# Queries and keys of an attention kernel: transposed in fp32 and split into parts from PSUM

## The chip, the core and the metric

The kernel runs on one core of a Trainium2 chip. A core has a matrix engine, TensorE (PE in the profile; its weight loads are listed apart as PEld), three engines for elementwise work, VectorE (DVE), ScalarE (ACT) and GpSimd (POOL), and a queue, SyncE (SP), that issues the DMAs here. PE writes only to PSUM, from which DVE and ACT read. The metric is the device time of one execution in microseconds (us), lower is better.

## The reference

One inference step of a four-layer backbone with 640 tokens (128 context tokens and 512 latent ones) of width 1024, 16 query heads and 4 key heads of 64. What matters of a layer:

```python
u = rms_norm(h, norm_pre[l]) * (1 + scl) + shift
p = u @ w_in_l
q, k, v, z = split(p)                       # 16 heads of q, 4 of k and v, gate z
q = rms_norm(q, q_g); k = rms_norm(k, k_g)  # per head
q, k = apply_rope(q), apply_rope(k)         # layers 0, 1 and 3, latent tokens
s = einsum('bqhgd,bkhd->bhgqk', q * scale, k)
o = softmax(s) @ v                          # over latent keys and cached context keys
h = h + gate * rms_norm((o * silu(z)) @ w_out_l, norm_post[l])
```

Layers 0 and 3 attend to all keys, layer 1 to a band, layer 2 to a neighbourhood on a grid. The 128 context tokens attend only to themselves; their keys and values are outputs too. The keys of an earlier context come from the input `cache_k`.

## The kernel before

Everything is fp32. A matrix product is made of products in the matrix engine's type F32R: a value is split into a high part, rounded to F32R, and a low part, the rest. For the scores the parts lie on the 128 rows that PE sums over: a query head of 64 is stacked as 64 rows of high parts and 64 rows of low parts, and a key head lies twice on the 128 rows, once in high parts (`kst[:, g, 0]`) and once in low parts (`kst[:, g, 1]`). So two matmuls per block of scores sum all four products.

A layer runs in stages: keys and values of five token tiles of 128 (`kv_chunk`); then two chunks of 8 query heads. A chunk makes its queries tile by tile (`q_chunk`: projection L497, headnorm, rotation, and then the parts), the gate `z` (L634), the attention of four pairs of heads (scores L698 or L724, transposed probabilities L773, product with values L780) and the heads of the context tokens (L800, L826, L834). The second chunk has two other key heads: their six tiles are stacked into `kst` anew (L1000), from `kn2`, where `kv_chunk` kept them. There is one buffer `kst` at a time; the output phase (L901 and what follows) borrows it for its gate rows. Last comes the output projection.

How parts are made before: for a query tile (L610 to L623), twice four heads, ACT rounds them into the first half of `hl` (L613), DVE or POOL subtracts to get the low parts into the other half (L615), PE transposes the four heads of 128 columns in F32R (L620), and ACT or DVE copies 512 elements per row from PSUM to the query tile `q` (`evac`, L256). For a key tile (`k_stack`, L538) ACT rounds two heads, doubled by a broadcast (L544), DVE or POOL subtracts (L545), PE transposes four pieces of 128 columns in F32R (L553), and ACT or DVE copies 512 elements to `kst`.

The order of the work is not written by hand. `Sched.emit` (L126) is a planner that runs when the program is built: each operation has a list of engines it may run on with an assumed duration, the operations it depends on, the buffers it needs, and a priority; the planner takes the one that can start first and emits a fixed order for each engine. PSUM is given out as two double tiles `S` and four tiles `B` (L227); tiles `cap_...` limit how much is in flight. Durations `P(336, tr, "R")`, `As(256, ...)` and the like are the planner's, in ns and elements. Each engine then executes its list in order and waits on semaphores.

## Time and profile before

| | |
|---|---|
| median of 3 runs | 1398.39 us (1394.93 to 1403.29) |
| the profiled execution | 1400.58 us, its span 1398.5 us |
| PE busy | 1357.7 us, 97% |
| DVE busy | 954.7 us, 68% |
| ACT busy | 758.6 us, 54% |
| POOL busy | 266.8 us, 19% |
| mean share of the DMA engines busy | 32% |
| mean granted clock of PE | 0.998 |

The profile is of one execution. The busy time of an engine is the union of its instructions; PE's matmuls overlap, so a listed duration of one of them is longer than what it adds, which is seen from the starts of the runs that follow each other in the timeline. A line of the page's part 5 or of the groups says how long an engine was idle just before those instructions and which instruction ended that wait.

### The profile page before, as it was taken

How to read it: one execution, taken by the hardware profiler on the slowest of the kernel's cores; microseconds unless marked ns; L12 is line 12 of the kernel's file. 1: busy time of each engine (PE TensorE's matmuls, PEld its weight loads, DVE VectorE, ACT ScalarE, POOL GpSimd, SP SyncE). 2: the span in 40 equal slices, each digit the busy share in tenths (PEclk: the TensorE clock that was granted, in tenths of full speed). 3: DMA queues.
4: the chain of work that ended last, by engine and by line, in shares of the span. 5: the costliest groups of instructions: out<-in, count | busy, mean ns of one | idle time of the engine just before them, and what ended most of it. 6: DMA issues, size and time to landing. Idle time of an engine off the chain costs nothing.

```text
span 1398.5 us, 25496 instructions
## 1 busy us (share of the span) xinstructions
PE 1357.7 (97%) x9464; PEld 1122.3 (80%) x9464; DVE 954.7 (68%) x2300; ACT 758.6 (54%) x1854; POOL 266.8 (19%) x306
## 2 busy tenths in 40 slices
PE   6999999999999999999999999999999999999998
PEld 3788887888778887887878888888778888778876
DVE  4777667765587786777486676578488876577653
ACT  4556565554355565666354567468345555465641
POOL 1122012010032102201033541441033210021100
PEclk9999999999999999999999999999999999999999
DMA  8522222224532402324542522342633210111032
GB/s 305 175 69 84 61 91 84 69 87 140 181 115 67 147 30 91 125 92 161 161 125 73 157 57 91 98 141 85 196 126 101 91 53 10 61 52 41 31 123 103
DMA packets 73323, 145.11 MB, mean 104 GB/s; under 512 B 8752, under 2 KB 13936, under 8 KB 73200
## 3 DMA queue, kind: packets, MB, share of 16 engines
q1 hardware_dynamic: 73200, 143.50, 31.6%
q8 instruction: 74, 1.21, 0.4%
...
## 4 chain that ended last, share of the span: by engine, by line
PE 83%; DVE 6%; ACT 4%; DMA 3%; issue 3%; POOL 0%; SPq 0%; DVEq 0%; POOLq 0%; ACTq 0%
PE B L497 21%; PE B L634 14%; PE B L780 8%; PE B L773 8%; PE S L901 8%; PE B L901 6%; PE S L698 5%; PE S L724 4%; PE B L383 3%; PE B L620 2%; PE S L497 1%; DVE w L262 1%; DMA raw<-in_w_mod 1%; DMA raw<-in_w_in 1%; PE B L451 1%
## 5 line engine op out<-in xcount | busy, mean ns | idle before, releaser
L307 POOL TENSOR_TENSOR sm<-sm,mhalf 128x1 f32<-128x1 f32 (+2 forms) x100 | 122.1, 1223 | 573.2 <-DVE sm L302 291.5
L497 PE MATMUL B<-w,uB 128*128 128x512 f32 x816 | 207.4, 401 | 0.0
L256 ACT ACTIVATE pt<-B 128x512 f32<-128x512 f32 (+1 forms) x228 | 126.9, 570 | 121.0 <-PE B L773 110.8
L497 PEld LDWEIGHTS B<-w,uB 128*128 128x128 f32 x816 | 149.2, 188 | 31.8 <-DVE uB L262 0.4
L634 PE MATMUL B<-uB,w 128*128 128x384 f32 x768 | 166.0, 348 | 0.6 <-DVE gate L642 0.3
L773 PE MATMUL B<-ident,p 128*128 128x128 f32 x1088 | 159.4, 276 | 3.1 <-ACT pt L256 2.3
L261 ACT ACTIVATE w<-raw 128x512 fp32r<-128x512 f32 x224 | 135.0, 627 | 30.2 <-PE B L901 8.0
L773 PEld LDWEIGHTS B<-ident,p 128*128 128x128 f32 x1088 | 125.1, 141 | 23.7 <-issue 13.6
L262 DVE TENSOR_TENSOR w<-raw,w 128x512 fp32r<-128x512 f32 x193 | 130.5, 700 | 13.0 <-ACT w L261 12.4
L497 PE MATMUL B<-w,uA 128*128 128x512 f32 x528 | 135.1, 403 | 1.1 <-DVE pt L256 0.8
L703 ACT ACTIVATE p<-S,sm 128x640 f32<-128x640 f32 x128 | 101.3, 794 | 59.6 <-DVE sm L701 54.6
L780 PE MATMUL B<-pt,vt 128*64 128x256 f32 (+1 forms) x1152 | 133.0, 376 | 0.0
L634 PEld LDWEIGHTS B<-uB,w 128*128 128x128 f32 x768 | 129.6, 188 | 3.7 <-issue 1.5
L701 DVE TENSOR_REDUCE sm<-S 128x1 f32<-128x640 f32 x128 | 102.7, 819 | 37.7 <-PE S L698 36.8
L634 PE MATMUL B<-uA,w 128*128 128x256 f32 x768 | 117.6, 290 | 0.3 <-DVE modc L394 0.3
L497 PEld LDWEIGHTS B<-w,uA 128*128 128x128 f32 x528 | 96.4, 188 | 24.7 <-DVE w L262 2.1
L780 PEld LDWEIGHTS B<-pt,vt 128*64 128x64 f32 x1152 | 77.5, 137 | 46.0 <-issue 11.4
L634 PEld LDWEIGHTS B<-uA,w 128*128 128x128 f32 x768 | 102.5, 189 | 3.4 <-issue 1.8
L658 DVE TENSOR_SCALAR p<-p,sm 128x640 f32<-128x640 f32 (+2 forms) x197 | 96.9, 506 | 6.6 <-DVE sm L657 0.5
L698 PE MATMUL S<-kst,q 128*128 128x320 f32 x512 | 96.8, 320 | 2.9 <-ACT p L703 2.8
L658 POOL TENSOR_SCALAR p<-p,sm 128x640 f32<-128x640 f32 (+2 forms) x59 | 44.0, 751 | 284.3 <-DVE sm L657 236.4
L737 ACT ACTIVATE p<-p,sm 128x512 f32<-128x512 f32 (+1 forms) x128 | 83.9, 657 | 6.4 <-DVE sm L735 6.3
...
## 6 DMA issues: line engine op xcount, KB each, us to landing
...
```

The costliest lines, as they stand in the source:

```text
L256: alts = {"A": Ap(n, lambda e: e.activation(out(), in_(), AF.Copy)), "V": V(n, lambda e: e.tensor_copy(out(), in_()))}
L261: S.op([As(n, lambda e: e.activation(h(), src(), AF.Copy))], r, w)
L262: f = lambda e: e.tensor_sub(l(), src(), h().bitcast(F32))
L307: S.op([("G", 395 + 157 * n, lambda e: e.tensor_tensor(r.ap, v.ap, mhalf.ap.to_broadcast([128, n]), op=OP.pow), "pow")], r=[v, mhalf], w=[r])
L497: e.matmul(ps(), t.ap[:, s, k, off:off + 128], W[k].ap[:, w], start=k == 0 and i == 0, stop=k == 7 and i == 2)
L634: e.matmul(ps.ap[:, 0:w], W[k].ap[:, wi, 128 * f:128 * f + 128], t.ap[:, s, k, :], start=k == 0 and i == 0, stop=k == 7 and i == 2)
L658: f = lambda e, i=i, p=p, w=w: e.tensor_scalar(p.ap[:, 0:w], p.ap[:, 0:w], rs.ap[:, i:i + 1], 1.0, op0=OP.mult, op1=OP.mult)
L698: e.matmul(ps.ap[:, b, 0:320], Q[t + 1].ap[:, hh], kst.ap[:, g, s, 320 * b:320 * b + 320], start=s == 0, stop=s == 1)
L701: S.op([V(640, lambda e, ps=ps, i=i: e.tensor_reduce(negm.ap[:, i:i + 1], ps.ap[:, :, 0:320], axis=AX.XY, op=OP.max, negate=True))], r=[ps ...
L773: e.transpose(pt.ap[:, c:c + 128], p.ap[:, b:b + 128], ident.ap)
L780: e.matmul(po.ap[64 * x:64 * x + 64, 256 * half + q0:256 * half + q0 + w], vt.ap[:, kt, 64 * g:64 * g + 64], sbt.ap[:, c0:c0 + w], start=f ...
L901: e.matmul(ps(), t.ap[:, s, k, off:off + 128], W[k].ap[:, w], start=k == 0 and i == 0, stop=k == 7 and i == 2)
```

## The change

For queries: the tile is transposed first, in fp32, four transposes of two heads each (128 columns) into one PSUM tile. After that head `2r` lies on partitions 0 to 63 and head `2r+1` on 64 to 127. For the even heads (x = 0), ACT rounds the 64 partitions out of PSUM into the upper 64 partitions of `q`, and DVE subtracts that from PSUM and writes the low part to the other 64 partitions. For the odd heads high and low part change places; both halves of a key are the same, so scores are computed as before. A score instruction now waits for the even or odd heads of its tile, instead of the first or second four.

For keys: the source is now the two heads doubled side by side, so that one transpose of 128 columns gives a head on both halves. The cached keys are loaded twice by DMA for that, `kn2` holds doubled heads, and a new copy `kd` (ACT or DVE) doubles the others. PE transposes two pieces of 128 columns in fp32 instead of four in F32R; ACT rounds 256 elements per row from PSUM into `kst`, and DVE subtracts into the low part.

```diff
--- before.py
+++ after.py
@@ -538,32 +538,28 @@
     @S.named("ks")
     def k_stack(src, srckey, kst, ct, cap=None):
 
-        hl = tmp([128, 2, 2, 2, 64], F32R)
         tc_ = [cap, kst] if cap else [kst]
-        s = lambda: src()[:, :, None, :].to_broadcast([128, 2, 2, 64])
-        S.op([As(256, lambda e: e.activation(hl.ap[:, 0], s(), AF.Copy))], r=[srckey], w=[(hl, 0)], touch=tc_)
-        f = lambda e: e.tensor_sub(hl.ap[:, 1], s(), hl.ap[:, 0].bitcast(F32))
-        S.op([G(256, f), VL(256, f)], r=[srckey, (hl, 0)], w=[(hl, 1)], touch=tc_)
-        ps = S.buf("B", [128, 512], F32R)
+        ps = S.buf("B", [128, 512])
 
         def tr(e):
-            for i in range(2):
-                for g in range(2):
-                    c = 128 * (2 * i + g)
-                    e.transpose(ps.ap[:, c:c + 128], hl.ap[:, i, g].rearrange("p a d -> p (a d)"), identr.ap)
-        S.op([P(336, tr, "R")], r=[hl, identr], w=[ps], touch=tc_)
-        evac(512, lambda: kst.ap[:, :, :, 128 * COL[ct]:128 * COL[ct] + 128],
-             lambda: ps.ap.bitcast(F32).rearrange("p (i g c) -> p g i c", i=2, g=2), [ps], [(kst, ct)])
+            for g in range(2):
+                e.transpose(ps.ap[:, 128 * g:128 * g + 128], src()[:, g].rearrange("p a d -> p (a d)"), ident.ap)
+        S.op([P(218, tr, "T")], r=[srckey, ident], w=[ps], touch=tc_)
+        v = lambda: ps.ap[:, 0:256].rearrange("p (g c) -> p g c", g=2)
+        d = lambda i: kst.ap[:, :, i, 128 * COL[ct]:128 * COL[ct] + 128]
+        S.op([As(256, lambda e: e.activation(d(0), v(), AF.Copy))], r=[ps], w=[(kst, ct)])
+        S.op([V(256, lambda e: e.tensor_sub(d(1), v(), d(0).bitcast(F32)))], r=[ps, (kst, ct)], w=[(kst, ct)])
 
     def new_kst():
         return S.buf("kst", [128, 2, 2, 768], F32R)
 
     @S.named("kv")
     def kv_chunk(l, tabs, W):
-        kst, vt, kn2 = new_kst(), S.buf("vt", [128, 6, 256]), S.buf("kn2", [128, 6, 2, 64])
-        ck = tmp([128, 2, 64])
-        S.op([D(64, lambda e: e.dma_start(ck.ap, a["cache_k"][0, l, :, 0:2]))], w=[ck], touch=[kst])
-        S.op([D(64, lambda e: e.dma_start(kn2.ap[:, 4], a["cache_k"][0, l, :, 2:4]))], w=[(kn2, 4)])
+        kst, vt, kn2 = new_kst(), S.buf("vt", [128, 6, 256]), S.buf("kn2", [128, 6, 2, 2, 64])
+        ck = tmp([128, 2, 2, 64])
+        for x in range(2):
+            S.op([D(64, lambda e, x=x: e.dma_start(ck.ap[:, :, x], a["cache_k"][0, l, :, 0:2]))], w=[(ck, x)], touch=[kst])
+            S.op([D(64, lambda e, x=x: e.dma_start(kn2.ap[:, 4, :, x], a["cache_k"][0, l, :, 2:4]))], w=[(kn2, 4)])
         S.op([D(128, lambda e: e.dma_start(vt.ap[:, KC, :], a["cache_v"][0, l].rearrange("t h d -> t (h d)")))], w=[(vt, KC)])
         k_stack(lambda: ck.ap, ck, kst, 4)
         for tau in range(5):
@@ -588,9 +584,13 @@
             if tau == 0:
                 S.op([D(128, lambda e, kn=kn: e.dma_start(o["nk"][0, l], kn.ap))], r=[kn])
                 S.op([D(128, lambda e: e.dma_start(o["nv"][0, l].rearrange("t h d -> t (h d)"), vt.ap[:, VC, :]))], r=[(vt, VC)])
-            S.op([As(128, lambda e, kn=kn, ct=ct: e.activation(kn2.ap[:, ct], kn.ap[:, 2:4], AF.Copy))], r=[kn], w=[(kn2, ct)],
+            two = lambda k0, kn=kn: kn.ap[:, k0:k0 + 2, None, :].to_broadcast([128, 2, 2, 64])
+            S.op([As(256, lambda e, two=two, ct=ct: e.activation(kn2.ap[:, ct], two(2), AF.Copy))], r=[kn], w=[(kn2, ct)],
                  touch=[cap])
-            k_stack(lambda kn=kn: kn.ap[:, 0:2], kn, kst, ct, cap)
+            kd = tmp([128, 2, 2, 64])
+            S.op([As(256, lambda e, two=two, kd=kd: e.activation(kd.ap, two(0), AF.Copy)),
+                  V2(256, lambda e, two=two, kd=kd: e.tensor_copy(kd.ap, two(0)))], r=[kn], w=[kd], touch=[cap, kst])
+            k_stack(lambda kd=kd: kd.ap, kd, kst, ct, cap)
         return kst, vt, kn2
 
     @S.named("qt")
@@ -607,20 +607,20 @@
                 qn = rope(xr, 8, tabs, "q", tau - 1, cap)
             else:
                 qn = gscale(xr, 8, tabs, 0, cap)
-            for i in range(2):
-                hl, pt = tmp([128, 4, 128], F32R), S.buf("B", [128, 512], F32R)
-                s = lambda i=i, qn=qn: qn.ap[:, 4 * i:4 * i + 4]
-                S.op([As(256, lambda e, s=s, hl=hl: e.activation(hl.ap[:, :, 0:64], s(), AF.Copy))], r=[qn], w=[(hl, 0)],
-                     touch=[cap])
-                f = lambda e, s=s, hl=hl: e.tensor_sub(hl.ap[:, :, 64:128], s(), hl.ap[:, :, 0:64].bitcast(F32))
-                S.op([G(256, f), VL(256, f)], r=[qn, (hl, 0)], w=[(hl, 1)], touch=[cap])
-
-                def tr(e, hl=hl, pt=pt):
-                    for h in range(4):
-                        e.transpose(pt.ap[:, 128 * h:128 * h + 128], hl.ap[:, h], identr.ap)
-                S.op([P(336, tr, "R")], r=[hl, identr], w=[pt], touch=[cap])
-                evac(512, lambda i=i, q=q: q.ap[:, 4 * i:4 * i + 4].rearrange("p h t -> p (h t)"),
-                     lambda pt=pt: pt.ap.bitcast(F32), [pt], [(q, i)])
+            pt = S.buf("B", [128, 512])
+
+            def tr(e, pt=pt, qn=qn):
+                for pr in range(4):
+                    e.transpose(pt.ap[:, 128 * pr:128 * pr + 128], qn.ap[:, 2 * pr:2 * pr + 2].rearrange("p h d -> p (h d)"),
+                                ident.ap)
+            S.op([P(436, tr, "T")], r=[qn, ident], w=[pt], touch=[cap])
+            for x in range(2):
+                hi, lo = (slice(0, 64), slice(64, 128))[::1 - 2 * x]
+                d = lambda rows, x=x, q=q: q.ap.rearrange("p (r x) t -> p x r t", x=2)[rows, x]
+                v = lambda hi=hi, pt=pt: pt.ap[hi].rearrange("p (r t) -> p r t", r=4)
+                S.op([As(512, lambda e, d=d, v=v, hi=hi: e.activation(d(hi), v(), AF.Copy))], r=[pt], w=[(q, x)], touch=[cap])
+                S.op([V(512, lambda e, d=d, v=v, hi=hi, lo=lo: e.tensor_sub(d(lo), v(), d(hi).bitcast(F32)))], r=[pt, (q, x)],
+                     w=[(q, x)], touch=[cap])
             Q.append(q)
         return Q
 
@@ -697,7 +697,7 @@
...
-                S.op([P(588, mm)], r=[(Q[t + 1], hh // 4)] + [(kst, x) for x in range(5)], w=[ps], seq="s")
+                S.op([P(588, mm)], r=[(Q[t + 1], hh % 2)] + [(kst, x) for x in range(5)], w=[ps], seq="s")
...
@@ -798,7 +798,7 @@
...
-            S.op([P(880, mm)], r=[(Q[0], gg), (kst, 5)], w=[ps], seq="s")
+            S.op([P(880, mm)], r=[Q[0], (kst, 5)], w=[ps], seq="s")
...
```

The planner then gives another order. On PE, in the stage of layer 0 that makes the first chunk's queries, before (`tmp` is `hl`, `q` and `kst` are the scores' inputs):

```order
L497 MATMUL B<-w,uB 128x512 x21
L620 MATMUL B<-identr,tmp 128x128 x4
L497 MATMUL B<-w,uB 128x512 x3
L620 MATMUL B<-identr,tmp 128x128 x4
L497 MATMUL B<-w,uB 128x512 x18
L620 MATMUL B<-identr,tmp 128x128 x4
L497 MATMUL B<-w,uB 128x512 x3
L620 MATMUL B<-identr,tmp 128x128 x4
L497 MATMUL B<-w,uB 128x512 x3
L698 MATMUL S<-kst,q 128x320 x4
L497 MATMUL B<-w,uB 128x512 x9
```

and now (`tmp` is the rotated query tile):

```order
L497 MATMUL B<-w,uB 128x512 x15
L614 MATMUL B<-ident,tmp 128x128 x4
L497 MATMUL B<-w,uB 128x512 x21
L614 MATMUL B<-ident,tmp 128x128 x4
L497 MATMUL B<-w,uB 128x512 x9
L698 MATMUL S<-kst,q 128x320 x4
L497 MATMUL B<-w,uB 128x512 x12
L614 MATMUL B<-ident,tmp 128x128 x4
L497 MATMUL B<-w,uB 128x512 x9
L698 MATMUL S<-kst,q 128x320 x4
L497 MATMUL B<-w,uB 128x512 x6
```

Two groups of four transposes per token tile, with projection or other matmuls between them, became one group of four.

On PE at the start of layer 1, where the cached keys are stacked, before (`tmp` are the parts of key tiles):

```order
L497 MATMUL B<-w,uA 128x512 x12
L497 MATMUL B<-w,uB 128x512 x18
L553 MATMUL B<-identr,tmp 128x128 x4
L497 MATMUL B<-w,uB 128x512 x3
L553 MATMUL B<-identr,tmp 128x128 x4
L497 MATMUL B<-w,uB 128x512 x15
L451 MATMUL B<-ident,p 128x128 x8
```

and now (the first `tmp` is the DMA's tile of cached keys):

```order
L497 MATMUL B<-w,uA 128x512 x12
L546 MATMUL B<-ident,tmp 128x128 x2
L497 MATMUL B<-w,uB 128x512 x18
L546 MATMUL B<-ident,tmp 128x128 x2
L497 MATMUL B<-w,uB 128x512 x18
L451 MATMUL B<-ident,p 128x128 x8
L497 MATMUL B<-w,uB 128x512 x6
```

The first transposes of a key tile moved from behind the first 18 projection matmuls of `uB` to a place ahead of them. On SP the load of the cached keys stands in the same place, before:

```order
L959 DMA xs_4274<-q 128x1024
L322 DMA raw<-in_w_in 128x512 x2
L565 DMA tmp<-in_cache_k 128x128
L322 DMA raw<-in_w_in 128x512
L590 DMA out_nv<-vt 128x256
L589 DMA out_nk<-tmp 128x256
```

and now:

```order
L959 DMA xs_4149<-q 128x1024
L322 DMA raw<-in_w_in 128x512 x2
L561 DMA tmp<-in_cache_k 128x2x64 x2
L322 DMA raw<-in_w_in 128x512
L586 DMA out_nv<-vt 128x256
L585 DMA out_nk<-tmp 128x256
```

It became two DMAs, one after the other, between the same weight loads.

On PE at the second chunk's keys of layer 0, before:

```order
L800 MATMUL S<-kst,q 128x128 x8
L780 MATMUL B<-pt,vt 64x256 x10
L553 MATMUL B<-identr,tmp 128x128 x24
L834 MATMUL B<-pt,vt 64x128 x4
L383 MATMUL B<-raw,cpad 32x128 x16
```

and now (`kn_441` is the buffer `kn2`):

```order
L800 MATMUL S<-kst,q 128x128 x8
L780 MATMUL B<-pt,vt 64x256 x10
L546 MATMUL B<-ident,kn_441 128x128 x12
L834 MATMUL B<-pt,vt 64x128 x4
L383 MATMUL B<-raw,cpad 32x128 x16
```

24 F32R transposes in a row became 12 in fp32, in the same place, and they read `kn2` itself.

## Rows read from the trace of the kernel before

**Rows 1.** The page: part 1, the busy time of each engine with its share of the span and its instructions; and the first line of part 4, the chain of work that ended last by engine, in shares of the span.

```profile
PE 1357.7 (97%) x9464; PEld 1122.3 (80%) x9464; DVE 954.7 (68%) x2300; ACT 758.6 (54%) x1854; POOL 266.8 (19%) x306
...
PE 83%; DVE 6%; ACT 4%; DMA 3%; issue 3%; POOL 0%; SPq 0%; DVEq 0%; POOLq 0%; ACTq 0%
```

**Rows 2.** Windows by stage: the stretch in us from the span's start, its length, then for each engine the busy time and (x) its instructions, the granted clock of PE, the share of the DMA engines and GB/s. The first chunk of queries of layer 0, the attention that follows, and the stage of layer 0's second chunk of keys and queries.

```profile
84.00:116.00 32.00, 31.84 (x238) 28.11 (x241) 26.68 (x54) 19.67 (x42) 8.95 (x7) 1.00 0.31 100
116.00:193.00 77.00, 77.00 (x661) 66.37 (x651) 54.65 (x113) 48.51 (x113) 8.91 (x10) 1.00 0.20 63
193.00:246.00 53.00, 49.86 (x346) 40.91 (x342) 34.05 (x71) 26.71 (x61) 11.70 (x8) 1.00 0.27 89
```

**Rows 3.** Timeline of PE in the first query stage of layer 0: start in us, length of the merged run, engine, line, operation, output and inputs, shape, count. L497 are projection matmuls, L620 the F32R transposes of query parts, four to a group.

```profile
86.83 4.43 PE L497 MATMUL B<-w,uB 128*128 128x512 f32 x18
91.10 0.46 PE L620 MATMUL B<-identr,tmp 128*128 128x128 f32 x4
91.39 0.93 PE L497 MATMUL B<-w,uB 128*128 128x512 f32 x3
92.16 0.47 PE L620 MATMUL B<-identr,tmp 128*128 128x128 f32 x4
92.46 0.93 PE L497 MATMUL B<-w,uB 128*128 128x512 f32 x3
```

**Rows 4.** Timeline of PE at the start of layer 1, same columns; the last one of a line is the idle time before it and what ended that. L451 are fp32 transposes of normalized rows, four to a group; L497 with uA and uB are the projection of keys and values of the first two and the last three token tiles.

```profile
393.41 0.60 PE L451 MATMUL B<-ident,p 128*128 128x128 f32 x4
393.77 3.05 PE L497 MATMUL B<-w,uA 128*128 128x512 f32 x12
396.66 0.60 PE L451 MATMUL B<-ident,p 128*128 128x128 f32 x4
...
402.40 3.05 PE L497 MATMUL B<-w,uA 128*128 128x512 f32 x12
405.29 4.39 PE L497 MATMUL B<-w,uB 128*128 128x512 f32 x18
```

**Rows 5.** Groups of instructions by line and shape over the whole span: line, engine, operation, names, shapes, count | busy us, mean ns of one | idle before and what ended it. Splitting of queries (L613, L615) and keys (L545), their transposes (L620, L553) and copies out of PSUM (L256), and two DVE operations of 512 elements with (L510) and without (L528) an operand in PSUM.

```profile
L256 ACT ACTIVATE q<-B 128x512 fp32r<-128x512 f32 x78 | 45.0, 595 | 31.9 <-PE B L620 31.6
...
L620 PE MATMUL B<-identr,tmp 128*128 128x128 f32 x320 | 36.1, 243 | 3.0 <-ACT pt L256 1.4 <-DVE tmp L615 1.3 <-DVE gate L642 0.4
...
L615 DVE TENSOR_TENSOR tmp<-tmp 128x256 fp32r<-128x256 f32 x78 | 32.2, 435 | 12.9 <-ACT tmp L613 12.7
...
L613 ACT ACTIVATE tmp<-tmp 128x256 fp32r<-128x256 f32 x80 | 29.5, 410 | 68.1 <-DVE tmp L534 41.9 <-DVE tmp L528 26.0
...
L510 DVE TENSOR_TENSOR tmp<-B,sm 128x512 f32<-128x512 f32 x40 | 27.5, 688 | 41.0 <-POOL sm L307 40.9
...
L256 ACT ACTIVATE kst<-B 128x512 fp32r<-128x512 f32 x44 | 25.4, 597 | 14.1 <-PE B L553 13.4
...
L553 PE MATMUL B<-identr,tmp 128*128 128x128 f32 x192 | 21.9, 246 | 3.8 <-ACT pt L256 1.9 <-DVE gate L642 0.7 <-DVE sm L806 0.4
...
L528 DVE TENSOR_TENSOR tmp<-tmp 128x512 f32<-128x512 f32 x24 | 16.8, 699 | 0.3
...
L545 DVE TENSOR_TENSOR tmp<-kn,tmp 128x256 fp32r<-128x256 f32 x22 | 9.7, 504 | 0.0
...
L545 DVE TENSOR_TENSOR tmp<-tmp 128x256 fp32r<-128x256 f32 x23 | 9.6, 420 | 4.2 <-ACT tmp L544 4.0
```

**Rows 6.** Timeline around the cached key tile in layers 0 to 3, all engines, same columns: the DMA's issue on SP's queue (L565), ACT's rounding of that tile (L544), and in layers 2 and 3 the projection matmuls that PE was in.

```profile
37.47 0.33 SPq L565 DMA_DIRECT2D tmp<-in_cache_k  x1
...
43.09 0.42 ACT L544 ACTIVATE tmp<-tmp 128x256 fp32r<-128x256 f32 x1 [2.59 <-DMA tmp<-in_cache_k]
...
402.67 0.42 SPq L565 DMA_DIRECT2D tmp<-in_cache_k  x1
...
407.23 0.42 ACT L544 ACTIVATE tmp<-tmp 128x256 fp32r<-128x256 f32 x1 [1.28 <-DMA tmp<-in_cache_k]
...
725.43 0.43 SPq L565 DMA_DIRECT2D tmp<-in_cache_k  x1
...
727.01 2.98 PE L497 MATMUL B<-w,uB 128*128 128x512 f32 x12
...
728.77 0.42 ACT L544 ACTIVATE tmp<-tmp 128x256 fp32r<-128x256 f32 x1 [0.36 <-DMA tmp<-in_cache_k]
...
1049.60 0.42 SPq L565 DMA_DIRECT2D tmp<-in_cache_k  x1
...
1051.18 2.97 PE L497 MATMUL B<-w,uB 128*128 128x512 f32 x12
...
1052.62 0.42 ACT L544 ACTIVATE tmp<-tmp 128x256 fp32r<-128x256 f32 x1
```

**Rows 7.** Timeline of PE at the second chunk of keys in layer 3: L553 are the F32R transposes of keys, L780 the product of probabilities and values.

```profile
1191.76 0.53 PE L553 MATMUL B<-identr,tmp 128*128 128x128 f32 x4 [1.56 <-ACT pt L256]
1192.60 0.53 PE L553 MATMUL B<-identr,tmp 128*128 128x128 f32 x4 [0.30 <-ACT pt L256]
1193.05 3.76 PE L780 MATMUL B<-pt,vt 128*64 128x256 f32 x20
```

**Rows 8.** Two windows of 1 us there, with the columns of rows 2.

```profile
1191.00:1192.00 1.00, 0.24 (x3) 0.24 (x3) 1.00 (x4) 1.00 (x5) 0.00 (x0) 1.00 0.00 0
...
1194.00:1195.00 1.00, 1.00 (x8) 0.59 (x6) 0.05 (x1) 0.92 (x6) 0.00 (x0) 0.50 0.00 0
```

More of the change, by code (lines that the diff above doesn't have):

```diff
@@ L724, in mm @@
                             e.matmul(ps.ap[:, i, o:o + n], Q[t + 1].ap[:, hh], v(s), start=s == 0, stop=s == 1)
-                S.op([P(w * 0.88 + 14, mm)], r=[(Q[t + 1], hh // 4)] + [(kst, x) for x in BAND[t]], w=[(ps, i)], seq="s")
+                S.op([P(w * 0.88 + 14, mm)], r=[(Q[t + 1], hh % 2)] + [(kst, x) for x in BAND[t]], w=[(ps, i)], seq="s")
                 bb, bap = bias[t]
```

## The prediction

> **What bounds the kernel now.** I read the page's busy shares and chain of waits first, then the windows by stage, then TensorE's timeline inside three stages. The reader should see in [rows 1] that TensorE (PE) is busy for 97% of the span and holds 83% of the chain that ended last, while DVE (68%) and ACT (54%) have room. [rows 2] show the same in a stage: while the queries of layer 0 are made (84 to 116 us) PE is busy 31.84 of 32 us and DVE 26.68. So a us taken from PE counts nearly in full as long as PE isn't made to wait, and work that moves between DVE and ACT counts only where it makes PE wait. DVE at 83% in that stage is the engine to watch.
>
> **The change part by part.**
>
> PE, removed. A query tile needs two groups of four F32R transposes, a key tile one: 320 and 192 instructions [rows 5], so 80 and 48 groups. One group costs less than its listed 243 ns each suggests, because they overlap. In [rows 3] the matmuls behind a group begin 0.29 and 0.30 us after it began. The matmuls ahead of it tell whether it starts late: 18 take 4.27 us, 0.237 each, so three need 0.71, and three took 0.77. A group is 0.30 to 0.36 us; I take 0.31, since other stretches of this kind read as the lower end.
>
> PE, added. A query tile gets one group of four fp32 transposes, a key tile one of two: 40 groups and 48. The kernel before has fp32 transposes of the same size. In [rows 4] a group of four lets the next matmuls begin 0.36 us later (393.41 to 393.77); the 12 matmuls up to the next group took 2.89 us where 12 at 0.237 need 2.84, so the front costs 0.05, and up to 0.08 if the rate of other stretches is taken. That is 0.41 to 0.44, I take 0.435. A group of two is taken as half of that, 0.20 to 0.22; I take 0.22.
>
> The sum on PE: queries 40 x (2 x 0.31 - 0.435) = 7.4 us, keys 48 x (0.31 - 0.22) = 4.3 us, together **-12 us**. By the ends: 40 x (0.60 - 0.44) + 48 x (0.30 - 0.22) = 10 us, and 40 x (0.72 - 0.41) + 48 x (0.36 - 0.20) = 20 us.
>
> DVE and ACT. From [rows 5]: DVE loses 78 subtractions of a query's low part (32.2 us), 45 of a key's (19.3) and the six copies from PSUM that fell to it (6 x 0.69), 55.6 us in all. It gains 80 subtractions of 512 at 0.69 and 48 of 256 at 0.42, 75.4 us. The new order also puts some 20 pieces of optional work on it that POOL or ACT did, about 10 us at 0.5 to 0.7 each. So DVE rises by about 30 us, to some 984, 70% of the span. ACT loses 80 roundings of queries (29.5), 122 copies out of PSUM (45.0 + 25.4), 48 roundings of keys like the first (48 x 0.41) and 20 copies half as wide (an estimate of 0.3 each from the 410 ns of the full width), 126 us; it gains 80 x 0.595 for queries and 88 x 0.41 for keys, 84. It falls by about 40. I price both at nothing: in the attention stages (116 to 193 us) PE is busy all 77 us and DVE 54.65 [rows 2], and there is room. In a query stage five tiles add 5 x (2 x 0.69 - 2 x 0.435) = 2.6 us to DVE's 26.68 of 32, which makes 91%. What it costs if that cover is gone is the third rival. Operations on 64 partitions are not in this trace; what is bounded is the number of elements in a row, 512, and I take them as long as those of 128 partitions. Half the time would take 28 us from DVE and change PE by nothing.
>
> On that subtraction the trace shows 688 ns for 512 elements with an operand in PSUM and 699 ns for both in SBUF [rows 5], so I charge nothing for moving it to PSUM. The Trainium skill (Perfetto Trace Analysis, section Optimizing Scalar/DVE Operations) speaks against the change here: about 60 ns of access overhead for DVE on SBUF and 125 on PSUM. By it the 128 subtractions would cost 8 us more DVE time, an estimate from that page, and the third rival would have 38 us to draw on instead of 30; the rows don't agree.
>
> The wait that is added. Before, the cached key tile went from its DMA to ACT, then DVE, then PE. ACT could stand still for it without PE noticing. Now PE transposes the DMA's tile itself, so PE waits for the DMA, and all its queued matmuls wait behind that. The DMA can start only when the tile of keys is free, at the end of a layer, and there are now two in a row on SP, 0.42 us apart [rows 6]. From SP's issue to ACT's use it took 5.62 us in layer 0, 4.56 in layer 1, 3.34 in layer 2 and at most 3.02 in layer 3 [rows 6]. In layer 1 the order puts the transposes right behind the 12 matmuls of [rows 4], at 405.29 us; the first half lands near 407.2, the second 0.42 later: PE stands 2.3 us. In layers 2 and 3 they come behind six of the 12 matmuls that began at 727.01 and 1051.18 [rows 6], so at 728.4 and 1052.6; with 3.34 + 0.42 us the data is there at 729.2 and 1053.4: 0.8 us each. In layer 0 the second half is issued behind a 512 KB weight piece, about 41.4 us, and lands between 44.4 and 47; PE reaches it near 44, both estimates from the place of the two in their queues. I take 1.5. Together **+5 us**; from 0 (all land in time) to 9 (5.6 us everywhere in layer 0 and 1, and a fall of the clock on top).
>
> The second chunk's keys. At the middle of each layer six key tiles are transposed in a row. In layer 3 PE stood 1.56 and 0.30 us ahead of them [rows 7]; its granted clock was 0.50 (1.2 of 2.4 GHz) at 1194 us, after it had been busy for 0.24 of the us from 1191 [rows 8], and 20 matmuls of the attention took 3.76 us [rows 7]. Now nothing has to be made first. But a PSUM buffer is then held by 0.41 on ACT and 0.42 on DVE one after the other, where one copy of 0.60 freed it; six tiles go through four buffers or fewer. Between -5 (all those waits and the slow clock gone) and +4 (one more us in each layer) I take **-1.5**.
>
> Other edits: key halves are doubled by ACT beforehand (in ACT's sum above); scores now wait for even or odd heads instead of the first or second four, which shifts no instruction's length.
>
> The sum: -12 + 5 - 1.5 = -8.5 us. It is made against the profiled execution, 1400.6 us (span 1398.5 and 2.1 around), which gives 1392. That execution stood 2.2 us above the median of the runs, 1398.4, so I forecast **1390 us**.
>
> **The rivals.**
> 1. The cached keys cost PE nothing, because the two small DMAs land sooner or PE arrives later than in my count. Then -12 - 1.5, 1385 us. For it: in layer 3 ACT didn't wait for the DMA at all. Against it: ACT did in the other three [rows 6]. The Trainium skill has a rule that would bring it about (DMA: Bandwidth & Descriptors, section Anatomy of one DMA — SWDGE (gpsimd) path, so for DMAs that GpSimd issues): a fixed 2.0 us plus the bytes. By it layer 1's first half would be there at 404.7, before PE. The rows say 3.0 to 5.6 us for SP's DMAs, so I give it no more than a quarter.
> 2. The gain is given back by the new order: a query tile now holds one PSUM buffer through two ACT copies and a DVE subtraction (0.6 + 0.6 + 0.69 us) where each half was free after one copy of 0.60. If PE waits 0.15 to 0.2 us more on each of the 40 tiles, 6 to 8 us go, and the time is 1397. For it: PE already stands for such a copy now and then (0.30 us at 1192.60) [rows 7]. Against it: half as many buffers are asked for.
> 3. Slower than before: in the query stages DVE becomes what PE waits for. The mechanism is the chain of each tile, where reduction, scaling, rotation and now two 0.69 us subtractions stand behind each other on one engine at 91%. It decides when more than 8.5 of the 30 us that DVE gains come to stand on PE's path; at half of them, 15 us, the time is 1405, at all 1420. For it: 83% in [rows 2] is the share before. Against it: ACT is 40 us lighter and takes copies, and the second half of layer 0's queries is made in a stage where DVE is busy 34.05 of 53 us [rows 2].
>
> That the change doesn't do what it says would mean that an fp32 transpose costs PE as much as two of F32R; at 0.41 to 0.44 us a group [rows 4] excludes it.
>
> **How the numbers follow.** Forecast 0.45, first rival 0.25, second 0.18, third 0.12. About 0.5% (7 us: below 1391.4, above 1405.4) is what a measurement of this kernel can tell from no change. The forecast's own range is 1382 to 1398; it gives two thirds of its chance to faster and the rest to no change. The first rival gives 0.22 to faster, the second nearly all to no change, the third 0.10 to slower. With the tails: faster 0.53, the same 0.35, slower 0.12. The range for 8 in 10 runs from 1378 (the 20 us end of PE's gain, with half of the DMA waits) to 1402.
>
> **What would show it.** Right: PE's fp32 group of four lets the next matmuls begin 0.36 us later, PE's busy time falls by about 10 us, and the largest new PE wait is for the cached keys in layer 1, near 2 us. DVE's busy time is 975 to 990, ACT's near 718. Wrong: no PE wait for that DMA (first rival), or PE waits for DVE or for a PSUM buffer by the 64-partition operations in the query stages (second and third), or an operation on 64 partitions that takes other than 0.6 and 0.69 us.

## The result, and the profile after

The changed kernel takes 1413.45 us (median of 6 runs, 1407.35 to 1415.94), the kernel before 1398.37 in the same comparison (6 runs, 1394.93 to 1404.16). The ratio is 1.0092, 95% interval 1.0073 to 1.0112: **slower by some 13 us** (the medians lie 15 apart), where 1390 was forecast and the range ended at 1402. It is the third rival's side.

The page of the changed kernel, part 1 and the chain by engine, as in [rows 1]:

```profile
PE 1353.3 (96%) x9208; PEld 1104.8 (78%) x9208; DVE 983.8 (70%) x2313; ACT 721.4 (51%) x1753; POOL 251.6 (18%) x286
...
PE 77%; DVE 9%; DMA 4%; ACT 4%; issue 3%; POOL 1%; SPq 1%; DVEq 0%; POOLq 0%; ACTq 0%
```

DVE and ACT are about as busy as forecast (984 and 718 us). Yet the span rose from 1398.5 to 1412.3. Subtract PE's busy time from the span: PE stood idle for 40.8 us before and 59.0 after, 18.2 more; and its busy time fell by 4.4 us only.

The groups of the new operations, by line and shape, columns as in [rows 5]:

```profile
L634 PE MATMUL B<-uB,w 128*128 128x384 f32 x768 | 166.8, 350 | 4.2 <-DVE q L622 3.9 <-DVE gate L642 0.3
...
L622 DVE TENSOR_TENSOR q<-B,q 64x512 fp32r<-64x512 f32 x80 | 55.1, 689 | 25.6 <-ACT q L621 23.9
L621 ACT ACTIVATE q<-B 64x512 fp32r<-64x512 f32 x80 | 47.3, 592 | 43.6 <-PE B L614 42.9
...
L614 PE MATMUL B<-ident,tmp 128*128 128x128 f32 x160 | 25.3, 282 | 5.4 <-DVE tmp L528 4.4 <-ACT pt L256 0.5 <-DVE kst L551 0.4
...
L551 DVE TENSOR_TENSOR kst<-B,kst 128x256 fp32r<-128x256 f32 x48 | 19.2, 418 | 8.4 <-ACT kst L550 8.1
...
L550 ACT ACTIVATE kst<-B 128x256 fp32r<-128x256 f32 x48 | 17.6, 383 | 13.6 <-PE B L546 13.2
```

Operations on 64 partitions take 592 and 689 ns, as long as those on 128 (595 and 688 in [rows 5]). New is what stands behind the bar: DVE sat still for 25.6 us in front of the low halves (L622), 23.9 of them for ACT's high halves.

What PE waited for: engine, kind of PSUM tile, its line, the instruction waited for, us in total, times, longest.

```profile
PE B L614 <- DVE tmp L528: 4.4, 8, 0.8
PE B L634 <- DVE q L622: 3.9, 3, 1.3
PE B L546 <- DVE kst L551: 3.7, 6, 1.6
...
PE B L546 <- DMA tmp<-in_cache_k: 2.1, 3, 1.3
...
PE S L698 <- DVE q L622: 0.8, 2, 0.4
PE S L724 <- DVE q L622: 0.7, 2, 0.5
```

9.8 us of it is behind DVE's work on a query tile (L528 is the rotation's last addition). Before, PE stood 1.3 us behind the low parts of the queries (L615 in [rows 5]). The cached keys, the wait I feared, cost 2.1.

ACT and DVE on the second query tile of layer 0, timeline columns as in [rows 3]:

```profile
88.18 1.20 ACT L621 ACTIVATE q<-B 64x512 fp32r<-64x512 f32 x2 [2.66 <-PE B L614]
...
89.40 0.68 DVE L622 TENSOR_TENSOR q<-B,q 64x512 fp32r<-64x512 f32 x1 [1.37 <-ACT q L621]
90.12 0.69 DVE L510 TENSOR_TENSOR tmp<-B,sm 128x512 f32<-128x512 f32 x1
90.84 0.69 DVE L622 TENSOR_TENSOR q<-B,q 64x512 fp32r<-64x512 f32 x1
```

The first low half needs only the first high half, which is done at 88.8. It starts at 89.40, when **both** are done. So it is in 36 of the 40 tiles (median: 0.64 us after the first high half, 0.03 after the second); in the other four ACT's second half starts only after DVE's first low half has ended. In none of the 40 do ACT and DVE read the PSUM tile at the same time. A tile takes 2.64 us from the first half to the last (median). The planner counts 0.52 us for a high half and 0.60 for a low one, and lets the first low half run beside the second high one: 0.52 + 2 x 0.60 = 1.72 (1.83 with the 0.11 us that it adds between ACT's end and DVE's start).

The stage of the second chunk's keys in layer 2, on PE, before and after (L546 reads `kn2`):

```profile
855.63 0.63 PE L497 MATMUL B<-w,uA 128*128 128x512 f32 x2
856.10 0.79 PE L553 MATMUL B<-identr,tmp 128*128 128x128 f32 x8
856.73 1.63 PE L497 MATMUL B<-w,uA 128*128 128x512 f32 x6
858.20 0.80 PE L553 MATMUL B<-identr,tmp 128*128 128x128 f32 x8
858.84 1.64 PE L497 MATMUL B<-w,uA 128*128 128x512 f32 x6
860.32 0.46 PE L553 MATMUL B<-identr,tmp 128*128 128x128 f32 x4
...
863.37 1.74 PE L780 MATMUL B<-pt,vt 128*64 128x256 f32 x16
```

```profile
868.42 0.38 PE L546 MATMUL B<-ident,kn 128*128 128x128 f32 x2
870.38 0.44 PE L546 MATMUL B<-ident,kn 128*128 128x128 f32 x2 [1.58 <-DVE kst L551]
871.75 0.44 PE L546 MATMUL B<-ident,kn 128*128 128x128 f32 x2 [0.93 <-DVE kst L551]
873.00 0.41 PE L546 MATMUL B<-ident,kn 128*128 128x128 f32 x2 [0.81 <-DVE tmp L510]
873.24 0.70 PE L773 MATMUL B<-ident,p 128*128 128x128 f32 x4
...
879.34 3.25 PE L780 MATMUL B<-pt,vt 128*64 128x256 f32 x16
```

Before, the transposes lie between projection matmuls (L497) and PE stands for none of them. After, the last three come with no projection matmuls planned between, and PE stands for each. The windows there, columns as in [rows 2]:

```profile
868.00:873.00 5.00, 1.67 (x10) 0.85 (x8) 2.36 (x6) 1.64 (x4) 1.65 (x1) 1.00 0.00 0
873.00:878.00 5.00, 3.61 (x16) 2.45 (x16) 3.02 (x6) 2.41 (x5) 0.00 (x0) 0.57 0.00 0
878.00:883.00 5.00, 4.71 (x21) 2.89 (x22) 0.47 (x2) 0.84 (x2) 0.00 (x0) 0.50 0.00 0
```

PE is busy for 1.67 of 5 us, and then its granted clock is 0.50 (1.2 of 2.4 GHz); 16 matmuls of L780 take 3.25 us instead of 1.74. Over the span, leaving out the last few us of the run, windows of 1 us show 20.4 us at half the clock after (from 665, 873 and 1208 us) and 3.4 before. PE was busy in 18.1 of these 20.4 us and in all of the 3.4 before. Work takes twice as long there, so the slow clock adds 9.1 us to PE's busy time after and 1.7 before: without it, busy time would have fallen by about 12 us, not 4.4.

### The profile page after: what moved, and what is told of

It is laid out like the page before. It is cut to its first block, busy times and chain, and to the rows that moved or that the text cites. A ratio compares the mean times of both kernels' runs of the same rounds, so it can differ in the third digit from the quotient of the medians.

```text
span 1412.3 us, 24795 instructions
## 1 busy us (share of the span) xinstructions
PE 1353.3 (96%) x9208; PEld 1104.8 (78%) x9208; DVE 983.8 (70%) x2313; ACT 721.4 (51%) x1753; POOL 251.6 (18%) x286
## 4 chain that ended last, share of the span: by engine, by line
PE 77%; DVE 9%; DMA 4%; ACT 4%; issue 3%; POOL 1%; SPq 1%; DVEq 0%; POOLq 0%; ACTq 0%
PE B L497 17%; PE B L634 13%; PE B L780 9%; PE B L773 8%; PE S L901 8%; PE B L901 6%; PE S L698 5%; PE S L724 4%; PE B L383 3%; PE S L497 2%; DVE q L622 2%; DMA raw<-in_w_mod 1%; DMA raw<-in_w_in 1%; PE B L614 1%; ACT q L621 1%
## 5 line engine op out<-in xcount | busy, mean ns | idle before, releaser
L497 PE MATMUL B<-w,uB 128*128 128x512 f32 x816 | 204.7, 400 | 0.1
L256 ACT ACTIVATE pt<-B 128x512 f32<-128x512 f32 (+1 forms) x222 | 123.1, 568 | 119.6 <-PE B L773 100.9
L497 PEld LDWEIGHTS B<-w,uB 128*128 128x128 f32 x816 | 150.1, 188 | 32.7 <-DVE uB L262 0.5
L634 PE MATMUL B<-uB,w 128*128 128x384 f32 x768 | 166.8, 350 | 4.2 <-DVE q L622 3.9
L497 PE MATMUL B<-w,uA 128*128 128x512 f32 x528 | 135.6, 405 | 1.6 <-ACT pt L256 1.1
L634 PEld LDWEIGHTS B<-uB,w 128*128 128x128 f32 x768 | 131.0, 190 | 7.1 <-issue 5.5
L780 PE MATMUL B<-pt,vt 128*64 128x256 f32 (+1 forms) x1152 | 134.1, 378 | 0.0
L634 PE MATMUL B<-uA,w 128*128 128x256 f32 x768 | 119.7, 290 | 1.3 <-DVE w L262 1.2
L497 PEld LDWEIGHTS B<-w,uA 128*128 128x128 f32 x528 | 96.8, 189 | 26.2 <-DVE w L262 1.8
L780 PEld LDWEIGHTS B<-pt,vt 128*64 128x64 f32 x1152 | 78.2, 139 | 47.7 <-issue 12.7
L634 PEld LDWEIGHTS B<-uA,w 128*128 128x128 f32 x768 | 102.7, 189 | 4.9 <-DVE w L262 2.5
L658 DVE TENSOR_SCALAR p<-p,sm 128x640 f32<-128x640 f32 (+2 forms) x207 | 101.8, 507 | 6.3
L698 PE MATMUL S<-kst,q 128*128 128x320 f32 x512 | 96.9, 321 | 2.8 <-ACT p L703 1.9
L658 POOL TENSOR_SCALAR p<-p,sm 128x640 f32<-128x640 f32 (+2 forms) x49 | 37.1, 766 | 301.4 <-DVE sm L657 263.3
L506 ACT ACTIVATE tmp<-B 128x512 f32<-128x512 f32 (+1 forms) x56 | 30.0, 535 | 115.8 <-PE B L497 107.8
```

The lines of the kernel that those rows point to most:

```text
L256: alts = {"A": Ap(n, lambda e: e.activation(out(), in_(), AF.Copy)), "V": V(n, lambda e: e.tensor_copy(out(), in_()))}
L497: e.matmul(ps(), t.ap[:, s, k, off:off + 128], W[k].ap[:, w], start=k == 0 and i == 0, stop=k == 7 and i == 2)
L634: e.matmul(ps.ap[:, 0:w], W[k].ap[:, wi, 128 * f:128 * f + 128], t.ap[:, s, k, :], start=k == 0 and i == 0, stop=k == 7 and i == 2)
L658: f = lambda e, i=i, p=p, w=w: e.tensor_scalar(p.ap[:, 0:w], p.ap[:, 0:w], rs.ap[:, i:i + 1], 1.0, op0=OP.mult, op1=OP.mult)
L698: e.matmul(ps.ap[:, b, 0:320], Q[t + 1].ap[:, hh], kst.ap[:, g, s, 320 * b:320 * b + 320], start=s == 0, stop=s == 1)
L780: e.matmul(po.ap[64 * x:64 * x + 64, 256 * half + q0:256 * half + q0 + w], vt.ap[:, kt, 64 * g:64 * g + 64], sbt.ap[:, c0:c0 + w], start=f ...
```

## The experiments

Ratios are to the kernel before on the same chip. Where runs of different chips are compared and their medians and their ratios give different gaps, both are given. Lines of edited kernels are shifted by a few (L626 in e5 and e10 is L622).

**The two parts alone.** e1 has the new `q_chunk` and the old keys, e2 the new `k_stack` and `kv_chunk` and the old queries.

> The queries as in the changed kernel, the keys as before. Theory A (the query tiles: PE waits because high and low part of a tile now come one after the other from ACT and DVE out of one PSUM buffer): nearly all of the loss is here, 1406 to 1415 us, with PE waits for L619-L622's kind of subtraction of 4 us or more. Theory B (the keys of the second chunk: six tiles hold PSUM buffers through ACT and DVE, PE stands and its clock falls): PE's saving on queries shows, 1390 to 1397 us. Theory C (nothing of the new operations, only another order from the planner): no sum of the parts, either can be 5 us up or down.

> The keys as in the changed kernel, the queries as before. Theory A: a small gain or nothing, 1393 to 1399 us. Theory B: nearly all of the loss, 1406 to 1412 us, with two falls of the clock at the second chunk's keys in layers 2 and 3 (17 us at half clock in the changed kernel's profile, 3.4 in that of before).

e1: 1408.54 (ratio 1.006, 1.0038 to 1.0082). e2: 1399.6 (0.9997, 0.9983 to 1.0012). The loss sits in the queries. The keys alone are worth nothing, though PE's count gives them 4.3 us. The prediction's terms for the keys add up to -4.3 + 5 - 1.5 = -0.8 us, which agrees as a sum, by luck rather than term by term: in e2 PE waits 2.5 us for the cached keys, and it runs 10.2 us at half the clock before the end of the run (3.4 before).

**True durations.** The planner is told what the trace shows for the four operations.

```diff
-S.op([As(512, lambda e, d=d, v=v, hi=hi: ...)], r=[pt], w=[(q, x)], touch=[cap])
+S.op([("A", 600, lambda e, d=d, v=v, hi=hi: ..., "As")], r=[pt], w=[(q, x)], touch=[cap])
-S.op([V(512, ...
+S.op([("V", 690, ...
```

> The changed kernel, with the planner told for the new operations what the profile measured (600 and 690 ns for a query half instead of 519 and 598, 400 and 420 for a key tile instead of 306 and 332). Theory A: PE is planned to come later to what it waited for, 3 to 8 us come back, 1405 to 1410 us. Theory B: 2 to 5 us come back at the keys. Theory C: it differs by some us either way, since any change of the numbers is another order.

1409.24 (1.0064, 1.0042 to 1.0086): about 4 us back. PE's waits for L528 fell from 4.4 to 0.2 us, those for the low halves rose (L634 5.0, L724 2.4, L698 1.2).

**No dependence between the halves.** DVE subtracts the identity instead of ACT's high half, and the score instructions wait for the low part by itself.

```diff
-e.tensor_sub(d(lo), v(), d(hi).bitcast(F32)))], r=[pt, (q, x)],
+e.tensor_sub(d(lo), v(), ident.ap[hi][:, None, :].to_broadcast([64, 4, 128])))], r=[pt],
```

> The changed kernel, but DVE's query half doesn't wait for ACT's: it subtracts the identity instead of the high part, so the low parts of the queries are wrong, and the amount of work is the same. Theory A: if the serial chain is the cost, 6 to 12 us come back, 1402 to 1408 us; if DVE's load is the cost and not the chain, it stays at 1410 to 1415. Theory B: the keys' waits stay, 1409 to 1414 us.

1427.03 (1.0192, 1.017 to 1.0214): slower still, above every range given for it. Its groups:

```profile
L622 DVE TENSOR_TENSOR q<-B,ident 64x512 fp32r<-64x512 f32 x80 | 55.1, 689 | 51.0 <-ACT q L621 31.7 <-PE B L614 18.6
L621 ACT ACTIVATE q<-B 64x512 fp32r<-64x512 f32 x80 | 47.4, 593 | 69.7 <-DVE q L622 57.3 <-PE B L614 11.9
```

No result passes between the halves any more, and each engine waits for the other all the same. What they share is the PSUM tile. The planner now takes each low half to run beside the high halves, and is further off than before: PE's waits behind a query tile rose from 9.8 to 16.2 us (L614 behind L528 6.1, L724 5.3, L698 3.5, L634 1.3).

**The truth about the halves.** e5: true durations, and both low halves come after both high halves and depend on them. e6: the same with the old keys. e7: e5, with the second chunk's keys split ahead of the transposes as in the kernel before.

```diff
-S.op([V(512, ...)], r=[pt, (q, x)], w=[(q, x)], touch=[cap])
+S.op([("V", 690, ..., "V")], r=[pt, (q, 0), (q, 1)], w=[(q, x)], touch=[cap])
```

> As the changed kernel, but the planner is told what the trace of the changed kernel shows: 600 ns for a high half of a query tile, 690 for a low half (400 and 420 for a key tile), and that both low halves start after both high halves (in 36 of 40 tiles of the changed kernel DVE's first low half starts 0.03 us after ACT's second high half, 0.63 us after the first, and in the other 4 ACT's second half starts only after DVE's first: one engine at a time reads the PSUM tile). Same instructions. Theory A, the planner packs other work too tightly because it believes that a tile takes 1.72 us from the first half to the last (0.52 + 2 x 0.60) where the chip takes 2.64: with the truth told DVE no longer stands still in front of a low half (25.6 us in the changed kernel, falls below 8), and the time falls to 1398 to 1405. Theory B, the 2.64 us themselves, in which one of four PSUM buffers is held and the scores wait for the tile: the idle time only moves to PE, and the time stays at 1406 to 1412, as with the true durations alone (1409).

> Queries as in the changed kernel and planned with the true durations and order of their halves, keys as in the kernel before. Queries alone took 1408.5 against 1398.4 before. Theory A: 1393 to 1400. Theory B: 1404 to 1409.

> As e5, but the second chunk's keys (20 tiles of 44) are split on ACT and POOL before the transposes as in the kernel before. If the falls of the clock at the second chunk's keys come of the new chain transposes, ACT, DVE there (PE stood 1.58 and 0.93 us behind DVE's low part in the changed kernel, and the half clock there took 10.2 and 6.8 us), this is 3 to 6 us below e5, and only one stretch of 3.4 us at half the clock is left in the middle of the run. If they come of the gap that the projection's end leaves in any case, it equals e5 within 2 us.

e5: 1405.43 (1.005, 1.0035 to 1.0065), 6 us (ratios) to 8 us (medians) better than the changed kernel at the same matrix work, between theory A's end (1405) and theory B's beginning (1406). PE's waits behind a query tile on DVE fell from 9.8 to 4.9 us. DVE still sat still for 17.0 us in front of the low halves, not under 8: idle time of DVE is not the cost, PE's waits behind it are. e6: 1403.69 (1.0047, 1.0026 to 1.0068), 2 (ratios) to 5 us (medians) below e1 and between the two theories: the truth alone returns part of the loss. e7: 1406.19 (1.004, 1.0022 to 1.0059), as e5; with the old splitting too the clock falls at 868 us, for 10.2 us. So the fall does not need the new key chain. What e7 shares with the changed kernel is the order, with no other matmuls between the last transposes (L567 is e7's old key transpose, L803 the product of probabilities and values):

```profile
865.60 0.46 PE L567 MATMUL B<-identr,tmp 128*128 128x128 f32 x4
866.93 0.53 PE L567 MATMUL B<-identr,tmp 128*128 128x128 f32 x4 [0.88 <-ACT kst L256]
868.15 0.55 PE L567 MATMUL B<-identr,tmp 128*128 128x128 f32 x4 [0.69 <-ACT kst L256]
869.83 1.12 PE L796 MATMUL B<-ident,p 128*128 128x128 f32 x4 [1.12 <-DVE tmp L510]
...
876.56 2.91 PE L803 MATMUL B<-pt,vt 128*64 128x256 f32 x16
```

**A shorter hold.** The tile is copied to SBUF first and split from there.

```diff
+qs = tmp([128, 512])
+evac(512, lambda qs=qs: qs.ap, lambda pt=pt: pt.ap, [pt], [qs])
...
-v = lambda hi=hi, pt=pt: pt.ap[hi].rearrange("p (r t) -> p r t", r=4)
+v = lambda hi=hi, qs=qs: qs.ap[hi].rearrange("p (r t) -> p r t", r=4)
```

> As the changed kernel, but a query tile is first copied whole from PSUM to SBUF (0.60 to 0.69 us, ACT or DVE) and the four halves are made from there, the low ones on DVE or POOL: the PSUM buffer is held some 1.4 us after the transposes rather than 3.3, the chain to the finished tile is as long as before (0.65 + 0.6 + 0.69 + 0.69 = 2.6), ACT and DVE have 24 us more work together. Theory B (the hold): PE's waits for a buffer released by a low half go (3.9 us) and the time falls by 3 to 8 us from the changed kernel's 1413. Theory A (the planner's wrong picture): here the halves' real order is as planned, so it falls as well, to about 1405. If what costs is the work on DVE and ACT or the length of the chain to the scores: not below 1413.

1411.25 (1.0095, 1.0068 to 1.0123). PE's wait for buffers behind low halves is gone, and nothing is gained, so the hold was not the main cost, unless the added copies ate what it gave back. Theory A's 1405 did not come either; this planner still has the short durations. The timeline of its second tile:

```profile
90.26 1.29 ACT L623 ACTIVATE q<-tmp 64x512 fp32r<-64x512 f32 x2
90.92 0.69 DVE L624 TENSOR_TENSOR q<-tmp,q 64x512 fp32r<-64x512 f32 x1 [0.82 <-ACT q L623]
```

From SBUF, DVE starts at 90.92, 0.03 us after ACT's first half (0.63 of the 1.29 us), while the second still runs. In 34 of the 40 tiles an ACT and a DVE half overlap. The taking of turns belongs to the shared PSUM tile.

**Tables.** The planner's priorities (`ORDER`) had been chosen for the program before. e9 changes one number of it in the kernel before.

```diff
-ORDER = {'hn': -470, 'up': -310, 'pv': 20, 'nat': 90, ...
+ORDER = {'hn': -470, 'up': -310, 'pv': -40, 'nat': 90, ...
```

> The kernel before with one number of the planner's priority table changed (pv from 20 to -40), nothing else: the same instructions in another order. Theory L, luck of the plan: the table fits the old program, and any edit that lets the planner choose anew costs several us, mostly as stretches at half the clock: 1402 to 1410, granted clock 0.992 to 0.995. Rival, the changed query and key chains themselves are what costs: 1397 to 1401, the clock as before (0.998).

1396.14 (0.997, 0.9949 to 0.9992), a little faster. Theory L as I put it falls: a new order does not always cost. But one number moves the time by some 4 us, so single comparisons under the old table, e1 to e8, are known no better than that.

e10 to e12 have tables from one search (some 900 tables each, judged by the planner's own plan): e5's program, the kernel before, and the changed kernel with the planner's wrong picture. e10's edit, the others in the same way:

```diff
-ORDER = {'hn': -470, 'up': -310, 'pv': 20, 'nat': 90, 'tab': -80, 'un': -170, 'bt': -280, 'st': -780, 'out': 230,
-         'z': 90, 'og': -200, 'sc': 180, 'qt': -410, 'no': 180, 'ks': -170, 'mod': 160, 'w': -60}
+ORDER = {'hn': -430, 'up': -344, 'pv': -5, 'nat': 90, 'tab': -120, 'un': -210, 'bt': -255, 'st': -799, 'out': 230,
+         'z': 53, 'og': -200, 'sc': 192, 'qt': -450, 'no': 155, 'ks': -230, 'mod': 94, 'w': -66}
```

The other tables, from e11 to e16 without e13:

```diff
+e11 ORDER = {'hn': -470, 'up': -345, 'pv': 1, 'nat': 90, 'tab': -80, 'un': -110, 'bt': -280, 'st': -780, 'out': 190,
+             'z': 65, 'og': -200, 'sc': 205, 'qt': -350, 'no': 168, 'ks': -207, 'mod': 135, 'w': -35}
+e12 ORDER = {'hn': -470, 'up': -370, 'pv': -5, 'nat': 90, 'tab': -74, 'un': -170, 'bt': -280, 'st': -780, 'out': 230,
+             'z': 65, 'og': -40, 'sc': 180, 'qt': -416, 'no': 168, 'ks': -110, 'mod': 160, 'w': -6}
+e14 ORDER = {'hn': -458, 'up': -270, 'pv': -5, 'nat': 78, 'tab': -40, 'un': -170, 'bt': -280, 'st': -740, 'out': 205,
+             'z': 65, 'og': -188, 'sc': 180, 'qt': -444, 'no': 156, 'ks': -210, 'mod': 160, 'w': -12}
+e15 ORDER = {'hn': -482, 'up': -310, 'pv': 20, 'nat': 90, 'tab': -20, 'un': -145, 'bt': -305, 'st': -768, 'out': 230,
+             'z': 90, 'og': -194, 'sc': 186, 'qt': -476, 'no': 155, 'ks': -218, 'mod': 160, 'w': -6}
+e16 ORDER = {'hn': -462, 'up': -310, 'pv': 14, 'nat': 102, 'tab': -128, 'un': -170, 'bt': -280, 'st': -780, 'out': 224,
+             'z': 84, 'og': -200, 'sc': 220, 'qt': -425, 'no': 180, 'ks': -170, 'mod': 108, 'w': -66}
```

> e5 (the changed kernel with true durations and order of the halves) with a new priority table, found by trying 900 tables with the kernel's own planner and keeping the plan that ends first and leaves PE the fewest thin stretches. Theory L: the 12 us of PE time that the change removes come out after all, and the clock falls go: 1375 to 1392, granted clock 0.996 or more. Rival, the 3.3 us from a tile's transposes to its last low half bound the query stages whatever the order: stays at 1400 to 1406.

> The kernel before with a new table from the same search of the same length: says what a new table gives without the change. Theory L: it gains less than e10 does, 1380 to 1397, and stays 5 to 12 us above e10. Rival: e10 gains no more than this one, the two within 3 us of each other or e10 above.

> The changed kernel with a new priority table from the same search of the same length as e10 and e11, but the planner still believes the short durations and the parallel halves. If the planner's wrong picture of a query tile costs its 6 to 8 us under any table (theory A): 1380 to 1386, 6 to 12 above e10's 1374.4, with DVE standing still in front of the low halves for 15 us or more. If a fitting table alone is enough: 1373 to 1377.

e10: **1374.43** (0.9821, 0.9799 to 0.9842). e11: 1386.22 (0.9905, 0.9882 to 0.9928). e12: 1392.91 (0.9958, 0.9943 to 0.9972). Part 1 of the three pages, in this order:

```profile
PE 1335.2 (97%) x9208; PEld 1103.0 (80%) x9208; DVE 960.3 (70%) x2261; ACT 724.6 (53%) x1770; POOL 289.2 (21%) x321
```

```profile
PE 1348.9 (98%) x9464; PEld 1121.8 (81%) x9464; DVE 941.7 (68%) x2276; ACT 754.9 (55%) x1860; POOL 285.1 (21%) x324
```

```profile
PE 1347.3 (97%) x9208; PEld 1103.5 (79%) x9208; DVE 959.8 (69%) x2257; ACT 722.9 (52%) x1764; POOL 293.4 (21%) x331
```

e10 is 11.8 us faster than e11. Both have a fitted table, but only e10's planner also has measured durations, those of the new operations: e11's planner counts 0.31 us for ACT's rounding of half a query tile, which takes 0.41 ([rows 5]). What true durations would give the kernel before was not run. A fitted table without the truth is not enough: e12 is 6.7 us slower than e11, and above the range that either theory gave it.

PE is busy 13.7 us less in e10 than in e11, and its idle time nearly equal (36.8 of a span of 1372.0 and 34.5 of 1383.4). Neither falls to half the clock before the last 4 us. PE's waits behind a query tile on DVE, in e12 and then in e10 (L626 is L622):

```profile
PE B L614 <- DVE tmp L528: 4.5, 8, 0.8
PE B L634 <- DVE q L622: 1.2, 1, 1.2
PE S L724 <- DVE q L622: 0.5, 2, 0.2
```

```profile
PE S L702 <- DVE q L626: 0.2, 1, 0.2
```

In e10 DVE stands still in front of the low halves for 24.3 us, much as in the changed kernel, and a tile takes 3.36 us (median) from the first half to the last, longer than the changed kernel's 2.64. So a long chain costs PE next to nothing where the plan leaves room for it. The profiled span of e12 is 22.0 us longer than e10's, and 6.0 of that is these waits. Another 5.8 are waits for the loads of `in_w_mod` (L383, 7.6 us against 1.8), and 12.1 are busy time of PE at the same instructions, 3.4 of it by the slow clock; why the rest of it differs was not traced. The second chunk's keys of layer 2 in e10, with projection matmuls between them again:

```profile
845.02 0.92 PE L497 MATMUL B<-w,uA 128*128 128x512 f32 x3
845.78 0.38 PE L546 MATMUL B<-ident,kn 128*128 128x128 f32 x2
845.91 1.65 PE L497 MATMUL B<-w,uA 128*128 128x512 f32 x6
847.40 0.38 PE L546 MATMUL B<-ident,kn 128*128 128x128 f32 x2
```

**Each part, and the luck of the search.** e13: the new keys alone, with true durations, and e14: the new queries alone, with true durations and turns, each with its own table from the same search. e15 and e16: e10 and e11 searched from another seed. e13's table:

```diff
+ORDER = {'hn': -470, 'up': -376, 'pv': -5, 'nat': 90, 'tab': -27, 'un': -110, 'bt': -280, 'st': -768, 'out': 170,
+         'z': 59, 'og': -200, 'sc': 205, 'qt': -435, 'no': 161, 'ks': -110, 'mod': 75, 'w': -60}
```

> Keys of the change alone, with their true durations and a table from the same search as e10 and e11. If the 4.3 us that PE saves on the keys come out under a fitted table: 1380 to 1384, against 1386.2 for neither part. If the doubled copies, the DMA wait and the held buffers eat them: 1385 to 1390.

> Queries of the change alone, with true durations and order of the halves and a table from the same search. If the 7.4 us that PE saves on the queries come out: 1376 to 1381. If the longer chain of a tile eats them even when it is planned: 1384 or more.

> As e10, with the table that the same search finds from another seed. Luck of the search small: within 4 us of 1374.4. Large: up to 1386, as far off as e11.

> As e11, with the table that the same search finds from another seed. Luck of the search small: within 4 us of 1386.2, and above e15 by 8 to 16 us. Large: under 1380 or over 1392.

e13: 1379.33 (0.9865, 0.9846 to 0.9884). e14: 1379.13 (0.9866, 0.9844 to 0.9888). e15: 1377.05 (0.984, 0.9812 to 0.9868). e16: 1389.04 (0.993, 0.9909 to 0.995). Two seeds differ by about 3 us, in both pairs. With the second seed the change is worth 12.0 us (e15 against e16), as with the first. Against e11, each part alone gains 6 (ratios) to 7 us (medians) and both gain 12. For the queries that is near the 7.4 of PE's count; the keys gain more than their 4.3, and e13 ends just under the range given for it. With 3 us of luck in a search, neither part is measured more finely than that.

| | median us | PE busy | PE idle | half the clock before the end |
|---|---|---|---|---|
| before | 1398.4 | 1357.7 | 40.8 | 3.4 |
| changed | 1413.5 | 1353.3 | 59.0 | 20.4 |
| e5, truth, old table | 1405.4 | 1348.4 | 53.6 | 17.0 |
| e12, wrong picture, new table | 1392.9 | 1347.3 | 46.7 | 6.8 |
| e11, before, new table | 1386.2 | 1348.9 | 34.5 | 0 |
| e10, truth, new table | 1374.4 | 1335.2 | 36.8 | 0 |

## Why the prediction was wrong

**PE, -12 us: right in kind, a little small.** Behind an fp32 group of four the next projection matmuls begin 0.36 us later in the changed kernel (median, 0.35 to 0.41). PE's busy time is lower by 13.7 us (e10 against e11) and 17.5 us (e15 against e16). The sum took F32R groups at the low end of their range and fp32 groups near the high end. But PE's busy time also moves with the order at the same instructions (1357.7 us before, 1348.9 in e11), so these differences are not the transposes alone.

**DVE and ACT moves "at nothing": the step that failed.** For the queries the sum had -7.4 us of PE time and nothing for ACT and DVE; e1 measured a loss of 8 to 9 us. The sums of ACT's and DVE's work were right, and I judged them by their shares of a stage: 91% of a query stage, room elsewhere. The share did not decide it: over the span DVE is busy for 70% in the changed kernel and in e10 alike. I had written the chain of a tile down (two ACT halves, then DVE) for the buffer's hold only, and did not ask what the planner takes it for. It plans 1.7 to 1.8 us where the chip takes 2.64; engines run their lists in order, so DVE's next work (the next tile's rotation, L528) is late, and PE's transposes with it. PE's waits behind a query tile are 9.8 us in the changed kernel, 4.9 in e5 and 0.2 in e10. With the old table the wrong picture costs 6 to 8 us (changed against e5). With fitted tables e12 and e10 are 18 us apart, from one search each, and only 6 of that is traced to these waits. The rest of the loss under the old table, 6 to 7 us from e5 to the kernel before, goes when the table is fitted too (e10).

**Cached keys, +5: right in mechanism, too large.** PE stood for them in three layers, 1.29 us in layer 1 instead of 2.3, 2.1 in all, and in layer 0 none.

**Second chunk's keys, -1.5: wrong sign in the changed kernel.** I counted the rows of layer 3, where something went away, and not what happens to PE where no other matmuls are planned between. There PE runs 17.0 us at half the clock (from 873 and 1208 us) against 3.4 before, and was busy for 14.7 of them: some 6 us lost, and the waits in front of the transposes. The 3.4 us from 665 follow a wait of 2.7 us for a load of `in_w_mod`. For the fall in layer 2, e7 and e10 point to the order: the old way of splitting falls too, and the new one does not where projections lie between.

**The rivals.** The third gave the side and the engine, but by DVE's load, which is nearly as high in e10 (960 us, 70%), the fastest of all. The second, the hold, was 3.9 us of waits, and e8, with added copies, gained nothing without them.

**On the taking of turns.** In the changed kernel no ACT and DVE halves of one query tile in PSUM overlap, and in e4, where no result passes between them, none do either; there the trace puts 31.7 us of DVE's idle time and 57.3 of ACT's down to the other engine's half. The Trainium skill (PSUM — Partial Sum Buffer, section Terms) calls two engines at once in the same bank and the same 32 partitions an error, reads included, and says that different groups of 32 partitions may be accessed at once. ACT's second half and DVE's first read different ones, so by that page they need not wait. What makes them wait is thus in the program's semaphores, which follow the whole tile. That is argued, not shown: no run went without the wait, and none shows what the page states.

**On the cost of PSUM for DVE.** A subtraction of 64 x 512 took 689 ns out of PSUM in the changed kernel and 708 out of SBUF in e8. The Trainium skill's rule weighed ahead of the result (Perfetto Trace Analysis, section Optimizing Scalar/DVE Operations) is again not borne out.

**Still open:** how much of e2's nothing is the order. The 2.5 us of waits for the cached keys and 6.8 us more at half the clock, at most 3.4 us lost, are together more than the 4.3 that PE saves, and one number of a table moves 4 us. And e10 against e11 holds the kernel before to its old durations.
